# A hybrid mixer layer on one core: normalising the mixer's input early, SiLU in one instruction, and transposes by VectorE and DRAM

## The chip, the core and the metric

The kernel runs on one core of one Trainium2 chip. The metric is the device time of one execution in microseconds (us). The engines are named as the profile names them: PE is TensorE (matmuls, with PEld for its weight loads), DVE is VectorE, ACT is ScalarE, POOL is GpSimd and SP is SyncE, which here issues nearly all DMAs. PSUM is the accumulator memory that PE writes to, and its unit here is a bank of 128 x 512 fp32.

## The reference

One decoder layer on 512 tokens of width 1024, all in fp32:

```python
h = h + 0.5 * swiglu(rmsnorm(h, ffn1_norm[l]), ffn1_w_in[l], ffn1_w_out[l])
h = h + hybrid_mixer(rmsnorm(h, mix_norm[l]), w_in[l], ...)
h = h + 0.5 * swiglu(rmsnorm(h, ffn2_norm[l]), ffn2_w_in[l], ffn2_w_out[l])
return rmsnorm(h, final_norm)
```

The mixer projects the normalised input with one wide matrix and splits the columns:

```python
(hq, hf, hi, hg, gq, gk, gv, ga, gb, gz, gate_h, gate_g) = jnp.split(proj, offsets, axis=-1)
# HGRN2 branch, 8 heads
q_h = silu(hq) * HG_DK ** -0.5;  log_f, k_h from hf
o_h = rmsnorm(hgrn2_chunked(q_h, k_h, hi, log_f), hgrn_out_norm) * silu(hg)
# Gated DeltaNet branch, 8 q/k heads, 16 value heads
qkv = silu(causal_short_conv(concat([gq, gk, gv]), conv_w))      # 4 taps
q_g, k_g = l2norm per head;  beta = sigmoid(gb);  g = -exp(a_log) * softplus(ga + dt_bias)
o_g = rmsnorm(gated_delta_chunked(q_g, k_g, cv, beta, g), gdn_out_norm) * silu(gz)
y = sigmoid(gate_h) * (o_h @ w_branch_hgrn) + sigmoid(gate_g) * (o_g @ w_branch_gdn)
return y @ w_out
```

The delta rule inverts, for each chunk and value head, a unit lower triangular matrix `I + A`, where `A` comes from `k k^T`, beta and the decays. Then a recurrence over the chunks reads and updates a 128 x 128 state per head.

## The kernel before

**Layout.** Activations lie with channels on the 128 partitions and the 512 tokens along the free axis ("channel-major"). `h` holds 8 such tiles (`h[:, kt]`). Every large matmul is done in three passes of a split fp32: the weights become `whi` and `wlo`, the activations `uh` and `ul`, and `mm3` (lines 165 to 168) issues hi*hi, hi*lo and lo*hi. ACT makes `whi` (a cast) and DVE makes `wlo` (a subtraction) from each 256 KB slab that SP has loaded into one of three `raw` buffers. Six `whi`/`wlo` pairs let the slabs be made ahead of PE.

**Stages.** The first feed-forward layer ends near 358 us, the mixer follows up to about 1258 us, then the second feed-forward layer. In the mixer a product of one 128-column block of the weights takes 24 matmuls of 512 columns into one of the two `mm` banks. The letters of the string `DENSE` name these products: F and Q (forget gate and query of an HGRN2 head), B (value and output gate of two HGRN2 heads, tokens on partitions), D (the decays), k, q, v (inputs of the convolution), y (HGRN2 branch projection), z (output gate of two delta heads, tokens on partitions, matmuls of 256 columns). The 16 products `t` (merge gates) are fillers: `choose` takes one when nothing in `DENSE` may go, and keeps two back while something is left there.

**What sets the order.** The class `Desk` plans the mixer when the kernel is built. Each piece of work is a generator that asks for a buffer ("get"), an event ("on"), a time on an engine ("use") or a delay ("lag"). The planner keeps a modelled clock for each engine, gives the engine to the ready piece of the smallest rank, and the instructions come out in that order. On the chip each engine then runs its own list in order and waits on semaphores, so an engine whose next instruction is late holds back everything behind it. SP's DMAs are ordered in the same way.

**Normalisation.** The RMSNorm factor of each token is not ready when the mixer's products start. `uh` and `ul` therefore hold `h` times the norm's gain, without that factor. The function `norm` (lines 1962 to 1989) sums the squares, takes the power on POOL and spreads the factor over the partitions as `rbc`. Each product's result is multiplied by `rbc` when it leaves PSUM (lines 919, 990, 1008, 1218, 1601), or by `rcol`, the factor as a column, where tokens lie on partitions (lines 1027 and 1624).

**SiLU** is made from Tanh: ACT computes `th = tanh(x/2)`, DVE computes `(th + 1) * x`, and the factor 2 left over is taken out later (lines 999, 1234, 1626, and the constants 4.0 at lines 1175, 1288 and 1547).

**Transposes.** The delta rule needs keys and values with tokens on partitions, and its output goes back to channels on partitions. PE does these as four matmuls with an identity each: `ptk` (line 1264, key and query of each of 8 head groups), `ptv` (line 1372, 16 value heads), `pto` (line 1568, 16 outputs) and `pt` (line 1193, 8 HGRN2 outputs).

**Delta rule.** For head group `u` (two value heads): `conv` makes k, q and v; `norms` and `g_n` make the norms and the matrix `n2`; `g_b` writes the 32 x 32 diagonal blocks of `n2` to DRAM (`nb`, line 1343), reads them back broadcast into the one buffer `m` (line 1349), and POOL inverts them in 31 steps of two instructions (lines 1361 and 1362); `g_inv` builds the full inverse; `g_rec` runs the recurrence over four chunks, then normalises and gates the output (line 1560), transposes it and writes it to DRAM (`od`). `operand` reads it back and splits it for the last product, `closing`.

Of the kernel before, what the change touches and what calls it, by code (L numbers as in the profile page):

```python
# [24 lines left out]
HH = 8  # L25
# [16 lines left out]
EXTRA = ((1, 3, 5, 7), (1, 3, 5, 7), (1, 3, 5, 7), (5, 7))  # L42
# [82 lines left out]
def body(tc, xT, cst, sqc, hmask, dta, w1o, w1a, w2a, wt, wn, wab, wbh, wbg, wo, w1b, w2b, yT, dbg=None):  # L125
# [25 lines left out]
    rcol, rhalf = rcols[:, 0:4], rcols[:, 8:12]  # L151
# [665 lines left out]
def mixer(tc, mp, e):  # L817
# [3 lines left out]
    uh, ul, rbc, rcols, rcol, rhalf, h = (e[k] for k in ("uh", "ul", "rbc", "rcols", "rcol", "rhalf", "h"))  # L821
    psc, dr, dense, slab, wp, mm3, ux, hd, dbg = (
        e[k] for k in ("psc", "dr", "dense", "slab", "wp", "mm3", "ux", "hd", "dbg"))
    wt, wn, wab, wbh, wbg, wo, dta, psd = (e[k] for k in ("wt", "wn", "wab", "wbh", "wbg", "wo", "dtab", "psd"))
# [60 lines left out]
    od = dr.tile([VH, P, T], F32, name="od")  # L885


    D = Desk(wx0=1, wx1=1, wx2=1, wx3=1, mm=2, a=2, b=2, d=1, e=1, ta=TA, tm=6, thg=1, raw=RB, w=WB, n2=2, gz=2, fs=1, ut=1, t=3, kn=3, gm=1,
# [15 lines left out]

    def decays(pab):
# [6 lines left out]
        yield "on", "rbc"  # L912
# [5 lines left out]
        yield *V(512), 1  # L918
        dve.tensor_tensor(z, z, rbc[:64], op=ALU.mult)
# [65 lines left out]
    def h_q(i, pt):  # L985
        yield "get", "ta", 2
        yield "on", "rbc"
        yield *V(512), 1
        qs = ta("qs")
        dve.tensor_tensor(qs, pt, rbc, op=ALU.mult)  # L990
        D.put("mm")
        yield A(512)
        th = ta("th")
        act.activation(th, qs, AF.Tanh, scale=0.5)
        tag = ("fs", "ut")[i % 2]
        yield "get", tag, 1
        yield V(512)
        qq = hq[i] = place(tag, "qq", (P, NT, 192), 4)
        dve.scalar_tensor_tensor(qq[:, :, :P], v3(th, NT), 1.0, v3(qs, NT), op0=ALU.add, op1=ALU.mult)
        D.put("ta", 2)  # L1000
        D.fire(("Q", i))

    def h_f(i, pt):
        yield "get", "ta", 1
        yield "on", "rbc"
        yield *V(512), 1
        fs = ta("fs")
        dve.tensor_tensor(fs, pt, rbc, op=ALU.mult)
        D.put("mm")
        yield A(512)  # L1010
        act.activation(fs, fs, AF.Tanh, scale=0.5)
# [13 lines left out]
    def h_v(i, t, o):  # L1025
        yield A(300)
        act.activation(hv_[i][:, t], o, AF.Copy, scale=rcol[:, t:t + 1])
        if t == 3:
            D.fire(("V", i))

    def h_head(i):
# [143 lines left out]
        dve.tensor_scalar(rho, ss, 4.0 / P, 4.0 * EPS * 4.0 * P, op0=ALU.mult, op1=ALU.add)  # L1175
# [4 lines left out]
        yield V(4)  # L1180
        dve.tensor_tensor(rho, rho, rcol, op=ALU.mult)
# [7 lines left out]
        yield "get", "d", 1  # L1189
        yield T_(.46)  # L1190
        pt = ps("pt")
        for c in range(NT):
            pe.transpose(pt[:, c * P:(c + 1) * P], on[:, c], ident)
# [3 lines left out]
        yield A(560)  # L1197
        act.activation(oh, pt, AF.Copy, scale=gn)
        yield V(560)
        dve.scalar_tensor_tensor(ol, pt, gn, oh.bitcast(F32), op0=ALU.mult, op1=ALU.subtract)  # L1200
        D.put("d")
        D.put(tag_o)
# [9 lines left out]
    def conv(k, i, pt, out, n):  # L1212

        yield "get", "ta", 2
        yield *V(512), 1
        ci = ta("ci", (P, T + 32))[:, :T + 3]
        dve.memset(ci[:, :3], 0.0)
        dve.tensor_tensor(ci[:, 3:], pt, rbc, op=ALU.mult)
# [39 lines left out]
    def norms(u, i, kq, kn, sm):  # L1258
# [4 lines left out]
        for c in range(NT):  # L1263
            pe.transpose(pt[:, c * P:(c + 1) * P], kq[:, c, i], ident)
# [848 lines left out]
```

## Time and profile before

| | |
|---|---|
| median of 3 runs | 1624.95 us (1624.8 to 1631.92) |
| profiled execution, its own time | 1623.19 us |
| its span in the profile | 1621.4 us |
| busy share of the span: PE, DVE, ACT, POOL | 99%, 70%, 53%, 26% |
| granted PE clock, mean | 0.997 |
| HBM read, written | 197.45 MB, 17.07 MB |

The span runs from the first to the last instruction; the time of the run lies 1.8 us above it. A busy PE here means that a matmul is in flight. Matmuls overlap, so the price of one is the distance between the starts of two that follow each other and not its own duration.

### The profile page before, as it was taken

Reading aid. Unit: us, or ns where it says so; the run is one execution under the profiler, and the core shown is the slowest. Engines: PE = TensorE matmul, PEld = TensorE weight load, DVE = VectorE, ACT = ScalarE, POOL = GpSimd, SP = SyncE. Lnnn points to the kernel's source line nnn. Section 1 sums busy time; section 2 is a strip of 40 time slices with the busy share of each in tenths; the row PEclk is TensorE's granted clock in tenths of the full one; section 3 lists DMA queues with packets and bytes.
Section 4 is the critical chain, followed back from the end, with each engine's and each line's share of the span. In section 5 each row is a group of like instructions: output and inputs, shape, how many; then the busy total and the mean of one; then the engine's idle time right before and its main releaser. Section 6 shows DMA issues by size and latency. Waiting matters only on the chain.

```text
span 1621.4 us, 30263 instructions
## 1 busy us (share of the span) xinstructions
PE 1599.5 (99%) x11170; PEld 1408.9 (87%) x11170; DVE 1134.0 (70%) x2166; ACT 858.5 (53%) x1853; POOL 414.6 (26%) x744
## 2 busy tenths in 40 slices
PE   8999999999999999999999999999999999999997
PEld 7999998887878788888888988888888899999887
DVE  7877774547677778658888888755545877778353
ACT  7766663332434435456566565553325766667232
POOL 0222210101121221254571666510001322220012
PEclk9999999999999999999999999999999999999999
DMA  5988843532312222443323333445545888883343
GB/s 177 236 185 183 183 104 98 172 114 86 104 40 73 88 76 90 129 147 98 102 90 110 104 102 121 150 137 185 159 143 163 192 201 183 184 185 79 115 136 117
DMA packets 128165, 216.52 MB, mean 134 GB/s; under 512 B 21888, under 2 KB 27776, under 8 KB 128016
## 3 DMA queue, kind: packets, MB, share of 16 engines
q1 hardware_dynamic: 110448, 182.89, 35.6%
q0 software_dynamic: 17280, 31.46, 12.8%
q8 instruction: 88, 1.44, 0.4%
q14 instruction: 61, 0.50, 0.1%
q10 hardware_dynamic: 288, 0.22, 0.1%
HBM read 197.45 MB, written 17.07 MB: 132 GB/s over the span
## 4 chain that ended last, share of the span: by engine, by line
PE 92%; DMA 3%; issue 1%; ACT 1%; DVE 1%; POOL 0%; SPq 0%; DVEq 0%; ACTq 0%; POOLq 0%
PE pmm L166 16%; PE pmm L167 15%; PE pmm L168 15%; PE pnat L166 4%; PE pnat L168 4%; PE pnat L167 4%; PE pfa L166 3%; PE pfa L167 3%; PE pfa L168 3%; PE pfx L166 2%; PE pfx L168 2%; PE pfx L167 2%; PE pfy L168 2%; PE pfy L167 2%; PE pfy L166 2%
## 5 line engine op out<-in xcount | busy, mean ns | idle before, releaser
L166 PE MATMUL pmm<-uh,whi 128*128 128x512 f32 x632 | 264.4, 418 | 5.6 <-ACT whi L709 5.6
L1865 ACT CAST whi<-raw 128x512 fp32r<-128x512 f32 x226 | 140.1, 620 | 214.5 <-PE pmm L167 156.8
L1867 DVE TENSOR_TENSOR wlo<-raw,whi 128x512 fp32r<-128x512 f32 x226 | 160.6, 711 | 128.3 <-ACT whi L1865 121.8
L168 PE MATMUL pmm<-uh,wlo 128*128 128x512 f32 x632 | 248.2, 393 | 0.0
L167 PE MATMUL pmm<-ul,whi 128*128 128x512 f32 x632 | 247.9, 392 | 0.0
L420 DVE TENSOR_TENSOR sig<-h,sig 128x1024 fp32r<-128x1024 f32 x80 | 97.7, 1221 | 70.4 <-ACT sig L418 70.4
L166 PEld LDWEIGHTS pmm<-uh,whi 128*128 128x128 f32 x632 | 119.5, 189 | 27.1 <-ACT whi L709 5.6
L168 PEld LDWEIGHTS pmm<-uh,wlo 128*128 128x128 f32 x632 | 119.2, 189 | 26.3
L166 PE MATMUL pmm<-gh,whi 128*128 128x512 f32 (+1 forms) x374 | 140.9, 377 | 0.0
L168 PE MATMUL pmm<-gh,wlo 128*128 128x512 f32 (+1 forms) x374 | 140.9, 377 | 0.0
L167 PE MATMUL pmm<-gl,whi 128*128 128x512 f32 (+1 forms) x374 | 140.8, 377 | 0.0
L167 PEld LDWEIGHTS pmm<-ul,whi 128*128 128x128 f32 x632 | 119.7, 189 | 20.4 <-DVE ul L193 0.2
L418 ACT CAST sig<-h 128x1024 fp32r<-128x1024 f32 x80 | 83.9, 1049 | 88.1 <-PE pfa L168 85.1
L204 POOL TENSOR_TENSOR acc<-acc,sqt 128x512 f32<-128x512 f32 x18 | 24.1, 1338 | 376.4 <-ACT sqt L202 376.3
L166 PE MATMUL pnat<-whi,uh 128*128 128x256 f32 (+1 forms) x328 | 107.7, 328 | 0.0
L162 DVE TENSOR_TENSOR wlo<-raw,whi 128x512 fp32r<-128x512 f32 x74 | 54.9, 746 | 67.6 <-ACT whi L161 66.9
L168 PE MATMUL pnat<-whi,ul 128*128 128x256 f32 (+1 forms) x328 | 100.6, 307 | 0.0
L167 PE MATMUL pnat<-wlo,uh 128*128 128x256 f32 (+1 forms) x328 | 100.4, 306 | 0.0
L395 POOL DMA_DIRECT2D wlo<-w1b x63 | 54.5, 868 | 145.9 <-ACT s L470 101.3
L168 PE MATMUL pfa<-th,sig 128*128 128x256 f32 x320 | 90.9, 284 | 0.6 <-DVE sig L420 0.5
L166 PE MATMUL pfa<-th,sig 128*128 128x256 f32 x320 | 91.0, 284 | 0.4 <-ACT s L475 0.4
L167 PE MATMUL pfa<-tl,sig 128*128 128x256 f32 x320 | 90.7, 283 | 0.0
(489 smaller groups left out, 4566.1 us busy)
## 6 DMA issues: line engine op xcount, KB each, us to landing
raw<-wt SPq DMA_DIRECT2D x128, 256.0 KB
raw<-w1b SPq DMA_DIRECT2D x88, 256.0 KB
raw<-w1a SPq DMA_DIRECT2D x80, 256.0 KB
raw<-wn SPq DMA_DIRECT2D x64, 256.0 KB
wlo<-w1b POOLq DMA_DIRECT2D x63, 256.0 KB, 5.9
wlo<-w1a POOLq DMA_DIRECT2D x57, 256.0 KB, 5.5
raw<-w2b SPq DMA_DIRECT2D x45, 256.0 KB
raw<-w2a SPq DMA_DIRECT2D x40, 256.0 KB
```

The source lines that it names most:

```text
L162: dve.tensor_tensor(lo[:, :f], raw[:, :f], hi[:, :f].bitcast(F32), op=ALU.subtract)
L166: pe.matmul(pt, ah, bh, start=first, stop=False, **kw)
L167: pe.matmul(pt, ah, bl, start=False, stop=False, **kw)
L168: pe.matmul(pt, al, bh, start=False, stop=last, **kw)
L204: add.tensor_tensor(acc, acc, s, op=ALU.add)
L395: pool.dma_start(lo, src_, accum_op=ALU.add)
L418: act.copy(hl[:, 0:2], s)
L420: dve.tensor_tensor(hl[:, 2:4], s, hl[:, 0:2].bitcast(F32), op=ALU.subtract)
L1865: act.copy(hi, raw)
L1867: dve.tensor_tensor(lo, raw, hi.bitcast(F32), op=ALU.subtract)
```

## The change

The input of the mixer's products is normalised, all but four of them. A new product `S0` runs the four blocks F0, Q0, F1 and Q1 together on the input without the factor, with the eight input tiles in the outer loop and four banks (`mm` twice, `a` twice). Behind each of its eight steps, `renorm` rewrites that tile of `uh` and `ul` with the factor in. The product `B0` then runs over four banks with the same outer loop. All later results leave PSUM without a multiplication by `rbc` or `rcol`.

SiLU becomes one ACT instruction with the function Silu, in `h_q`, `conv`, `gate` and the new `zgate`. The convolution reads its input straight from PSUM: ACT makes the last tap, and three DVE instructions with shifted columns add the others, where the bank was free before after one DVE instruction.

Fifty groups of four PE transposes go: the keys and queries (16), the values (16), the delta outputs of the first seven head groups (14) and the outputs of the first four HGRN2 heads (4). In their place `turned` transposes 32 x 32 blocks on DVE and writes the tile to DRAM, and `regroup` reads it back with four DMAs whose runs are 32 fp32, that is 128 bytes. The gate `z` is now computed channel-major in 16 products of 512 columns, passed through Silu, kept in DRAM (`zd`), and multiplied in by `operand`; its 16 products join the 16 `t` as fillers, ahead of them. The delta outputs are scaled by their norm on ACT.

In the delta rule `n2` has three buffers instead of two, `m` has two instead of one, DVE makes `n2` from PSUM without the copy `gm`, and the two Exp of a head group stand next to each other on ACT.

```diff
 DENSE = (
-    "F0 Q0 F1 Q1 B0 F2 Q2 F3 Q3 B1 D0 F4 Q4 F5 Q5 B2 F6 Q6 F7 Q7 B3 "
-    "k0 q0 k1 q1 y0 y1 y2 y3 v0 v1 y4 y5 y6 y7 k2 q2 v2 v3 z0 k3 q3 v4 v5 z1 k4 q4 v6 v7 z2 "
-    "k5 q5 v8 v9 z3 k6 q6 v10 v11 z4 k7 q7 v12 v13 z5 v14 v15 z6 z7 "
+    "S0 B0 F2 Q2 F3 Q3 B1 D0 F4 Q4 F5 Q5 B2 F6 Q6 F7 Q7 B3 "
+    "k0 q0 k1 q1 y0 y1 y2 y3 v0 v1 y4 y5 y6 y7 k2 q2 v2 v3 k3 q3 v4 v5 k4 q4 v6 v7 "
+    "k5 q5 v8 v9 k6 q6 v10 v11 k7 q7 v12 v13 v14 v15 "
 )
-EXTRA = ((1, 3, 5, 7), (1, 3, 5, 7), (1, 3, 5, 7), (5, 7))
+EXTRA = ((), (1, 3, 5, 7), (1, 3, 5, 7), (5, 7))
...
+    def turned(x, src, mem, then=None, *arg):
+        yield V(512)
+        dve.transpose(v3(x, NT), v3(src, NT) if len(src.shape) < 3 else src)
+        if then is not None:
+            then(*arg)
+        yield S
+        sp.dma_start(mem, x)
+        yield "lag", LAG["out"]
+
+    def regroup(to, mem):
+        rows = mem.rearrange("(t s) (c b r) -> b s c t r", t=4, c=NT, b=4)
+        for b in range(4):
+            yield S
+            o = to[32 * b:32 * b + 32]
+            sp.dma_start(o.rearrange("p (c t r) -> p c t r", c=NT, t=4) if len(o.shape) < 3 else
+                         o.rearrange("p c (t r) -> p c t r", t=4), rows[b])
+        yield "lag", LAG["back"]
...
     def conv(k, i, pt, out, n):
-        yield "get", "ta", 2
-        yield *V(512), 1
-        ci = ta("ci", (P, T + 32))[:, :T + 3]
-        dve.memset(ci[:, :3], 0.0)
-        dve.tensor_tensor(ci[:, 3:], pt, rbc, op=ALU.mult)
-        D.put("mm")
-        yield A(512)
-        y = ta("cy")
-        act.activation(y, ci[:, :T], AF.Copy, scale=wc[0])
-        for j in range(1, 4):
-            yield V(550)
-            dve.scalar_tensor_tensor(y, ci[:, j:j + T], wc[j], y, op0=ALU.mult, op1=ALU.add)
-        yield A(512)
-        th = ci[:, :T]
-        act.activation(th, y, AF.Tanh, scale=0.5)
-        ...
-        dve.scalar_tensor_tensor(out, a, 1.0, b, op0=ALU.add, op1=ALU.mult)
+        yield "get", "ta", 1
+        yield *A(512), 1
+        y = ta("cy")
+        act.activation(y, pt, AF.Copy, scale=wc[3])
+        for j in range(1, 4):
+            yield *V(550), 1
+            dve.scalar_tensor_tensor(y[:, j:], pt[:, :T - j], wc[3 - j], y[:, j:], op0=ALU.mult, op1=ALU.add)
+        D.put("mm")
+        ...
+        if n:
+            act.activation(out, v3(y, n), AF.Silu)
+        else:
+            act.activation(y, y, AF.Silu)
+            D.start((4, k[1], 5), values_of(k, y))
...
     def norms(u, i, kq, kn, sm):
-        yield "get", "e", 1
-        pt = ps("ptk", "e")
-        for c in range(NT):
-            pe.transpose(pt[:, c * P:(c + 1) * P], kq[:, c, i], ident)
+        yield from turned(x, kq[:, :, i], kd[2 * u + i])
+        ...
+        yield from regroup(to, kd[2 * u + i])
...
-        yield "on", *([("P", u - 1)] if u else ["m"])
-        m = G["m"][0]
+        yield "on", *([("P", u - 2)] if u > 1 else [("m2", 0)] if u else ["m"])
+        m = G["m2" if u % 2 else "m"][0]
...
     def g_w(u, i, st):
-        pt = ps("ptv", "e")
-        for c in range(NT):
-            pe.transpose(pt[:, c * P:(c + 1) * P], vb[:, c], ident)
-        dve.tensor_tensor(vb, v3(pt, NT), bc(st["c2"][:, :, i], P), op=ALU.mult)
+        dve.tensor_tensor(vb, vb, bc(st["c2"][:, :, i], P), op=ALU.mult)
...
+    def send(u, i, o):
+        yield "get", "on", 1
+        x = places["on"]("on")
+        yield V(512)
+        dve.transpose(v3(x, NT), o)
+        D.fire(("R", u, i))
+        D.start((6, u), keep(od[2 * u + i], x, "on", ("od", 2 * u + i)))
...
+    def zgate(i, pt):
+        yield "get", "ta", 1
+        yield *A(512), 1
+        z = ta("zg")
+        act.activation(z, pt, AF.Silu)
+        D.put("mm")
+        D.start((6, i), keep(zd[i], z, "ta", ("z", i)))
...
     def operand(k, wait, get, make):
-        yield "on", ("od", k), *([("so", k - 2)] if k > 10 else [])
+        yield "on", ("od", k), *(["projected"] if k > 10 else [])
+        yield "on", ("z", k)
+        ...
-        sp.dma_start(og, od[k])
-        yield "lag", LAG["back"]
+        sp.dma_start(zg, zd[k])
+        yield from regroup(og, od[k])
+        yield *V(560), 1
+        dve.scalar_tensor_tensor(og, og, cs[:, C_GN:C_GN + 1], zg, op0=ALU.mult, op1=ALU.mult)
...
+    def renorm(kt):
+        yield "on", "rbc"
+        yield "get", "ta", 1
+        yield V(560)
+        w = ta("un")
+        dve.scalar_tensor_tensor(w, h[:, kt], cs[:, C_MX + kt:C_MX + kt + 1], rbc, op0=ALU.mult, op1=ALU.mult)
+        yield A(512)
+        act.copy(uh[:, kt], w)
+        yield V(512)
+        dve.tensor_tensor(ul[:, kt], w, uh[:, kt].bitcast(F32), op=ALU.subtract)
...
+            if k == "S":
+                yield "get", "mm", 2
+                yield "get", "a", 2
+                ps_ = [psd.tile(...) for _ in range(2)] + [ps("pmm", "a") for _ in range(2)]
+                for kt in range(KD):
+                    yield "on", ("slab", (x, kt))
+                    for o, pt in enumerate(ps_):
+                        yield T_(.69)
+                        mm3(pt, hi[:, c], lo[:, c], *ux(kt), kt == 0, kt == KD - 1)
+                    D.put("w")
+                    D.start((0, kt), renorm(kt))
+                for o, (th, lane) in enumerate(((h_f, "mm"), (h_q, "mm"), (h_f, "a"), (h_q, "a"))):
+                    D.start((5, n), th(o // 2, ps_[o], lane, True))
+                continue
```

More of the change, by code (lines that the diff above doesn't have):

```diff
@@ L911, in decays @@
         z2 = h[:16, 2]
-        yield "on", "rbc"
         yield A(512)
@@ L1188, in h_head @@
         D.fire(("o", i))
-        yield "get", "d", 1
-        yield T_(.46)
-        pt = ps("pt")
-        for c in range(NT):
-            pe.transpose(pt[:, c * P:(c + 1) * P], on[:, c], ident)
+        if i >= 4:
+            yield "get", "d", 1
+            yield T_(.46)
+            x = ps("pt")
+            for c in range(NT):
+                pe.transpose(x[:, c * P:(c + 1) * P], on[:, c], ident)
+        else:
+            yield "get", "ta", 1
+            x = ta("xo")
+            yield from turned(x, on, ohd[i], D.put, tag_o)
+            yield from regroup(x, ohd[i])
         gn = cs[:, C_HN:C_HN + 1]
@@ L1253, in g_e @@
             D.put("gb")
-            yield A(512)
+        yield "use", "ACT", 3.9
+        for i in range(2):
+            a = G["at"][u % 4 * 2 + i]
             act.activation(a, a, AF.Exp, scale=-1.0)
@@ L2005, in mixer @@
     D.start((6, 0), claim("t64", "t64", 2, (P, 4, 64), True))
+    D.start((6, 0), spare())
     D.start((6, 0), second())
```

375 lines of the change are left out of this document (204 added, 171 removed).

## The prediction

> **What bounds the kernel now.** I read the page first: the busy shares, the slices and the chain that ended last.
>
> ```profile
> span 1621.4 us, 30263 instructions
> PE 1599.5 (99%) x11170; PEld 1408.9 (87%) x11170; DVE 1134.0 (70%) x2166; ACT 858.5 (53%) x1853; POOL 414.6 (26%) x744
> PE   8999999999999999999999999999999999999997
> DVE  7877774547677778658888888755545877778353
> PE 92%; DMA 3%; issue 1%; ACT 1%; DVE 1%; POOL 0%; SPq 0%; DVEq 0%; ACTq 0%; POOLq 0%
> ```
>
> PE is busy in nearly every slice and makes 92% of the chain. The mixer may still have stages of its own, so the next view gives the busy time in stretches of it (columns: stretch, its length, then busy time of PE, PEld, DVE, ACT, POOL, granted clock, DMA share, GB/s). The last three rows are from a second such view over the delta rule alone.
>
> ```profile
> core 0: us, PE busy (x) PEld busy (x) DVE busy (x) ACT busy (x) POOL busy (x), PEclk, DMA share, GB/s
> 360.00:460.00 100.00, 100.00 (x819) 81.57 (x817) 72.00 (x188) 37.41 (x82) 17.20 (x21) 1.00 0.26 80
> 1060.00:1130.00 70.00, 69.09 (x412) 56.78 (x411) 39.03 (x89) 34.27 (x91) 4.13 (x4) 1.00 0.48 166
> sum 900.00, PE 898.66 PEld 757.35 DVE 649.33 ACT 446.48 POOL 284.89; mean PE 99.85 PEld 84.15 DVE 72.15 ACT 49.61 POOL 31.65
> ...
> 764.00:815.00 51.00, 51.00 (x408) 44.13 (x407) 44.79 (x104) 32.69 (x93) 28.75 (x65) 1.00 0.34 100
> sum 402.00, PE 401.56 PEld 349.30 DVE 314.77 ACT 236.28 POOL 215.56; mean PE 50.20 PEld 43.66 DVE 39.35 ACT 29.54 POOL 26.95
> ```
>
> Over the mixer's 900 us PE is busy for 898.66, at the full clock. So **PE's queue is the bound of the mixer**, and the change is worth what it takes out of that queue, less the waits that it puts in. DVE is next: over the eight periods of the delta rule (402 us) it is busy 314.77 / 402 = 78%, and up to 44.79 / 51 = 88%. POOL needs 27 us and PE 50 us per head group, so the inversions don't set the pace.
>
> The merge gates `t` tell how much room the delta chain has at its end. Their row gives the first and last of the 16:
>
> ```profile
> L1601 DVE TENSOR_TENSOR tg<-pmm,rbc x16: 674/684/693, 558.1 to 1128.3; 128x512 f32<-128x512 f32 x16
> ```
>
> The fillers last to 1128 us, until the closing product begins; PE has work in hand to the end.
>
> **Terms on PE.** A busy duration is not the price of a matmul; the distance of starts is. The groups of the transposes and one place each where they stand between dense matmuls (start, duration, what):
>
> ```profile
> L1568 PE MATMUL pto<-sq,on 128*128 128x128 f32 x64 | 9.7, 273 | 0.0
> L166 PE MATMUL pnat<-whi,uh 128*128 128x256 f32 x256 | 77.8, 304 | 0.0
> ...
> 719.26 0.39 PE L167 MATMUL pmm<-ul,whi 128*128 128x512 f32 x1
> 719.49 0.40 PE L168 MATMUL pmm<-uh,wlo 128*128 128x512 f32 x1
> 719.72 0.60 PE L1264 MATMUL ptk<-sq,h 128*128 128x128 f32 x4
> 720.08 0.48 PE L166 MATMUL pmm<-uh,whi 128*128 128x512 f32 x1
> 720.39 0.40 PE L167 MATMUL pmm<-ul,whi 128*128 128x512 f32 x1
> ...
> 781.83 0.28 PE L167 MATMUL pnat<-wlo,uh 128*128 128x256 f32 x1
> 781.95 0.28 PE L168 MATMUL pnat<-whi,ul 128*128 128x256 f32 x1
> ```
>
> Two dense matmuls of 512 columns stand 719.49 - 719.26 = 0.23 us apart (0.227 over longer runs). From 719.49 to 720.39 there are two of them and one group of four transposes: 0.90 - 2 x 0.227 = 0.446 us for the group. The change removes 50 groups: 16 `ptk`, 16 `ptv`, 14 of the 16 `pto`, 4 of the 8 `pt`. **That is 50 x 0.446 = 22.3 us.**
>
> The gate `z` has 768 matmuls of 256 columns, three passes of 256 (the `pnat` row), at 781.95 - 781.83 = 0.12 us: 92.2 us. In the new form it has 16 x 24 = 384 of 512 columns at 0.227: 87.2 us. **5.0 us less.** Nothing is added to PE. `S0` has the matmuls of F0, Q0, F1 and Q1, `B0` keeps its number, and fillers replace fillers. 22.3 + 5.0 = 27.3 us, all on the engine that sets the end.
>
> **The start of the mixer.** PE's first matmul there, the factor's copy, the first result that uses it, the convolution's steps and the weight cast:
>
> ```profile
> 358.08 0.39 PE L166 MATMUL pmm<-uh,whi 128*128 128x512 f32 x1
> ...
> L1987 ACT COPY rbc<-pbc x1: 587/587/587, 366.6 to 366.6; 128x512 f32<-128x512 f32 x1
> L1008 DVE TENSOR_TENSOR fs<-pmm,rbc x8: 671/687/692, 367.2 to 549.4; 128x512 f32<-128x512 f32 x8
> L1226 DVE SCALAR_TENSOR_TENSOR cy<-ci,cs,cy 128x512 f32<-128x512 f32 x96 | 72.9, 762 | 2.1 <-ACT cy L1223 0.7
> L1223 ACT ACTIVATE cy<-ci,cs 128x512 f32<-128x512 f32 x32 | 23.0, 721 | 7.9 <-DVE ci L1218 7.3 <-DVE x L1234 0.5
> L1218 DVE TENSOR_TENSOR ci<-pmm,rbc 128x512 f32<-128x512 f32 x32 | 22.0, 687 | 4.9 <-PE pmm L168 4.3
> L1865 ACT CAST whi<-raw 128x512 fp32r<-128x512 f32 x226 | 140.1, 620 | 214.5 <-PE pmm L167 156.8 <-PE pnat L168 19.2 <-issue 16.9
> ```
>
> `S0` runs from 358 us for 96 x 0.227 = 21.8 us, to 380. The factor is there at 366.6 + 0.6 = 367.2. A `renorm` is two DVE instructions and one on ACT, by the nearest rows 0.76 + 0.62 + 0.69 = 2.1 us, and needs its tile's step of `S0` done (2.7 us each). The first six follow the factor at DVE's 1.45 us each and are ready by 376; the last tile is free at 380 and ready near 383, while `B0` needs it only at its eighth step, 380 + 7 x 2.7 = 399. So PE doesn't wait for it. The cover is `B0`'s outer loop; without it the wait would be 2 to 3 us. One small loss: the second block of `S0` goes into the bank of the last product of the feed-forward layer after 0.7 us instead of 5.4 us, and that bank is free only after one DVE instruction of 0.69 us: 0.7 us. Head 1 starts about 15 us late, as its banks `b` hold `B0` until 402. That moves the heads, not PE, which has 32 fillers of 5.45 us to go on with.
>
> **The delta rule off PE.** Each transposed tile now costs one DVE transpose, one write, four reads. DVE has no 128 x 512 transpose in this profile; it lies between a plain 128 x 512 instruction and twice the largest transpose here:
>
> ```profile
> L1386 DVE STREAM_TRANSPOSE x<-gln 128x256 f32<-128x256 f32 x3 | 2.1, 708 | 0.0
> L1234 DVE SCALAR_TENSOR_TENSOR h<-ci,cy 128x512 f32<-128x512 f32 x12 | 8.3, 692 | 3.2 <-ACT ci L1229 2.9
> L1626 DVE SCALAR_TENSOR_TENSOR ggz<-thg,pnat 128x256 f32<-128x256 f32 x24 | 10.0, 417 | 3.8 <-ACT thg L1624 3.6
> L1560 DVE SCALAR_TENSOR_TENSOR on<-gat,sm,ggz 128x128 f32<-128x128 f32 x24 | 8.9, 416 | 0.1
> ```
>
> So 0.69 to 1.42 us; I take 1.1, as both ends are one element per lane and step with a strided source in the second. Per head group DVE gains six of them and two products in `operand`: 6 x 1.1 + 2 x 0.76 = 8.1 us (5.7 to 10.0). It loses, of four convolutions, the multiplication and the last step, 4 x (0.69 + 0.69); of `z`, four times 0.42; the eight gated scalings, 8 x 0.42; two of `gm`, which have the size of the 0.42 row: 5.5 + 1.7 + 3.4 + 0.8 = 11.4 us. DVE is lighter by 1.4 to 5.7 us of 39, so the engine next in line isn't made the bound. ACT takes the eight small scalings and gives back a copy of 512 columns for the keys and two for the outputs, about nothing in sum.
>
> SiLU and Exp may not share ACT's function table. The loads in this profile:
>
> ```profile
> 485.80 0.61 ACT L1865 CAST wx<-raw 128x512 fp32r<-128x512 f32 x1
> 486.43 1.28 ACT L931 ACT_TABLE_LOAD   x1
> 487.72 0.63 ACT L931 ACTIVATE h<-h 16x512 f32<-16x512 f32 x1
> ```
>
> Two loads per head group and a few around the decays are some 20 x 1.28 = 26 us (0 if no load is needed) on an engine busy 29.5 of 50 us; six slabs made ahead (6 x 2.7 = 16 us of PE) cover each. [...]
>
> The DMAs: a regroup moves 2048 runs of 128 bytes. The block writes of `g_b` have such runs. Two answers on the DMA queue, of 1017.6 to 1019.6 us (1104 of these runs) and of 1024.0 to 1030.6 us (reads from DRAM), and the issue on SP:
>
> ```profile
> DMA packets 1192, 0.31 MB, mean 156 GB/s; under 512 B 1104, under 2 KB 1104, under 8 KB 1192
> q1 hardware_dynamic: 1192, 0.31, 71.9%
> ...
> DMA packets 442, 0.95 MB, mean 144 GB/s; under 512 B 52, under 2 KB 171, under 8 KB 441
> q1 hardware_dynamic: 441, 0.94, 50.9%
> L1343 SPq DMA_DIRECT2D nb<-gn x32: 325/448/1347, 657.7 to 1017.7; - x32
> ```
>
> The first gives 2.0 x 0.719 x 16 / 1192 = 0.019 us of an engine per packet, the second 6.6 x 0.509 x 16 / 441 = 0.12. A regroup keeps the 16 engines for 2.5 us by the first and 15.6 by the second; I take the first, whose runs have the same size. Fifty of them are 125 us, on DMA engines at 26 to 48% in the mixer. SP issues some 290 DMAs more at 0.45 us, 130 us over 700 (1.35 us each, the longest of that row, would be 390 us). The waits behind a late regroup are DVE's or ACT's next slab, with 16 us of cover. I take **3 us** of new waits on PE in sum (0 to 25), some of it in the tail, where operands 11 to 13 are read back only when all products are done, and 11 is needed 4 x 2.7 + 2 = 13 us later, against some 10 us to fetch and make it.
>
> **Sum.** The profiled execution's 1623.2 us: 1623.2 - 22.3 - 5.0 + 0.7 + 3 = 1599.6 us. The median of the runs is 1.8 us above it: **1601 us**.
>
> **Rivals.** (a) *The banks are held too long: slower.* A convolution now frees its bank after 0.72 + 3 x 0.76 = 3.0 us in place of 0.69, and PE is back at that bank 24 x 0.227 = 5.45 us after the product's end. It decides when more than 2.4 us of other work come between on ACT and DVE. With DVE at 78 to 88%, two foreign instructions of 0.71 us ahead of each tap make 0.72 + 3 x (0.76 + 1.42) = 7.3 us, 1.8 us over, for 32 convolutions 58 us: 1601 + 58 = 1659 us. Against it: the taps have the highest rank in the plan, and small matmuls stand between the products. 9%. (b) *Short runs are slow to read: slower.* At 15.6 us a regroup takes 50 x 15.6 = 780 us of the DMA engines, more than the idle half of the mixer's 900, so the weights come late as well; it decides from some 9 us per regroup (450 us), and 50 times 1 us on PE is my price: 1601 + 50 = 1651 us. The rows of 0.019 us speak against it. 5%. [...] (c) *The gain is eaten by scattered waits*, no change: fifty round trips and 32 held banks each cost PE 0.3 us, 82 x 0.3 = 25 us, which is 1624 us. 12%. (d) *The change doesn't take PE's work away*, because the transposes only filled waits: the stretches show 1.3 us of idle PE in 900, so there were none to fill. 2%, 1623 us. (e) *Somewhat more*: the 1.3 us of idle PE goes as well and no new wait comes, 1601 - 3 - 1.3 = 1597 us; it is in the forecast's own range.
>
> **How the numbers follow.** Forecast with its own range of 1594 to 1612: 72%. Rivals (c) and (d) lie near 1624, (a) and (b) between 1635 and 1660. Each end leaves out about a tenth: 1593 to 1626. What a measurement can tell from no change is 0.5%, 8 us. Faster by more than that (under 1617): 72% and a part of (c), 0.77. Within: 0.11. Slower: 0.12.
>
> **What would show it.** The groups `ptk` and `ptv` gone, 8 matmuls of `pto` and 16 of `pt` left; PE's busy sum in the mixer down by 25 to 28 us at the same busy share. Wrong would be: PE idle ahead of `pmm` matmuls, released by DVE `cy` (rival a) or by DMA (rival b); idle PE near 380 us; fillers used up before the last recurrence, with PE idle between the last `t` and the closing product; a regroup over 5 us long.

## The result, and the profile after

The changed kernel takes 1616.03 us (median of 5 runs, 1612.69 to 1616.82) against 1624.95 us of the kernel before beside it. The ratio is 0.9937, with a 95% interval of 0.9925 to 0.9949. That is 8.9 us faster, where 24 us were forecast.

The page of the changed kernel: span, busy times, PE's slices, the packets, and the chain that ended last.

```profile
span 1614.9 us, 29415 instructions
...
PE 1580.5 (98%) x10586; PEld 1371.3 (85%) x10586; DVE 1076.1 (67%) x1970; ACT 872.8 (54%) x1905; POOL 388.3 (24%) x736
...
PE   8899999999999999999999999999999999999997
...
DMA packets 241538, 243.73 MB, mean 151 GB/s; under 512 B 128352, under 2 KB 134240, under 8 KB 241392
...
PE 83%; DMA 5%; ACT 4%; DVE 2%; SPq 2%; issue 2%; POOL 1%; POOLq 0%; ACTq 0%; DVEq 0%
```

PE lost 584 matmul records and 19 us of busy time. But it makes only 83% of the chain now, where it made 92%. DMA, ACT, DVE and SP's queue have come into it. The stretches of the mixer, as in the prediction's second view (the two worst of nine rows, and the sum):

```profile
660.00:760.00 100.00, 97.42 (x521) 79.50 (x521) 61.74 (x121) 57.30 (x128) 45.28 (x126) 0.98 0.62 179
...
960.00:1060.00 100.00, 94.51 (x603) 77.72 (x603) 57.07 (x133) 55.08 (x162) 47.75 (x127) 0.97 0.63 169
...
sum 900.00, PE 888.42 PEld 726.87 DVE 599.17 ACT 466.94 POOL 261.48; mean PE 98.71 PEld 80.76 DVE 66.57 ACT 51.88 POOL 29.05
```

PE is idle for 11.6 of 900 us, where it was idle for 1.3. Its clock isn't full in these two stretches either. The waits of PE in the delta rule (engine, line, what it waited for: sum, times, longest) name three places:

```profile
PE pks L1539 <- DVE s L1579: 3.8, 2, 3.0
PE pgq L1366 <- DVE gn L1374: 2.6, 1, 2.6
PE pog L1566 <- DVE gwe L1557: 2.5, 1, 2.5
```

Behind each of them stands a DMA. At the first (start, duration, line; in brackets the idle time and what ended it):

```profile
680.82 0.40 SPq L1902 DMA_DIRECT2D raw<-wt  x1
...
684.51 6.64 SPq L1902 DMA_DIRECT2D raw<-wt  x3
687.78 0.62 ACT L1945 CAST whi<-raw 128x512 fp32r<-128x512 f32 x1 [4.02 <-DMA raw<-wt]
...
688.43 0.69 DVE L1947 TENSOR_TENSOR wlo<-raw,whi 128x512 fp32r<-128x512 f32 x1 [3.95 <-ACT whi L1945]
...
690.72 0.85 DVE L1374 SCALAR_TENSOR_TENSOR gn<-pgq,sm,gat 128x128 f32<-128x128 f32 x3
```

ACT's cast at 687.78 needs the slab of weights that SP issued at 680.82 us. By the updates of its semaphore in the trace this slab is there at 687.68. ACT waits 4.02 us for it and DVE waits 3.95 us for ACT. The small `gn`, which PE's next matmul needs, stands behind that slab on DVE. At the second place (964 us) ACT's square of `norms` waits 3.9 us for a regroup. At the third (1009 us) DVE's product of `operand` waits 4.0 us for one. All three have the same form: an engine's list holds a late tile, and a small instruction of the delta chain is behind it.

Right after each of these waits PE's clock is halved for 3.4 us (columns as before; the clock is the third number from the end):

```profile
692.00:695.40 3.40, 3.40 (x9) 2.66 (x9) 1.89 (x7) 0.00 (x0) 2.69 (x10) 0.52 0.66 222
968.30:971.70 3.40, 3.40 (x39) 2.85 (x39) 2.65 (x10) 2.81 (x13) 2.77 (x9) 0.51 0.67 224
1012.70:1016.10 3.40, 3.40 (x9) 2.22 (x7) 2.91 (x7) 1.36 (x5) 2.93 (x7) 0.50 0.82 249
```

Each costs about 1.7 us, 5.1 us in sum. PE counts as busy then, so the busy time doesn't show it.

From the starts of the matmuls, the mixer (end of the first feed-forward layer to the first matmul of the last projection) took 856.7 us before and 848.0 us after: 8.6 us less instead of the 27.3 us that were forecast to leave PE's queue. Of the missing 18.7 us, 10.3 are idle PE (11.6 - 1.3) and 5.1 are half clock. The other 3.3 us show neither as idle time nor in the clock. Matmuls overlap (a dense one of 512 columns lasts 0.39 us, and the next starts after 0.23 us), so short delays can hide in a busy PE; whether the 3.3 us are such delays, or work that the forecast left out, isn't shown.

### The profile page after: what moved, and what is told of

It reads as the page before. It is cut to its first block, busy times and chain, and to the rows that moved or that the text cites. A ratio compares the mean times of both kernels' runs of the same rounds, so it can differ in the third digit from the quotient of the medians.

```text
span 1614.9 us, 29415 instructions
## 1 busy us (share of the span) xinstructions
PE 1580.5 (98%) x10586; PEld 1371.3 (85%) x10586; DVE 1076.1 (67%) x1970; ACT 872.8 (54%) x1905; POOL 388.3 (24%) x736
## 3 DMA queue, kind: packets, MB, share of 16 engines
q8 instruction: 83, 1.36, 0.3%
## 4 chain that ended last, share of the span: by engine, by line
PE 83%; DMA 5%; ACT 4%; DVE 2%; SPq 2%; issue 2%; POOL 1%; POOLq 0%; ACTq 0%; DVEq 0%
PE pmm L166 15%; PE pmm L167 15%; PE pmm L168 15%; PE pfa L166 3%; PE pfa L168 3%; PE pfa L167 3%; PE pfx L166 2%; PE pfx L167 2%; PE pfx L168 2%; PE pfy L168 2%; PE pfy L166 2%; PE pfy L167 2%; PE pnat L166 2%; PE pnat L168 2%; PE pnat L167 2%
## 5 line engine op out<-in xcount | busy, mean ns | idle before, releaser
L166 PE MATMUL pmm<-uh,whi 128*128 128x512 f32 x760 | 318.8, 420 | 6.8 <-ACT whi L709 5.5
L167 PE MATMUL pmm<-ul,whi 128*128 128x512 f32 x760 | 298.6, 393 | 0.5 <-DVE ul L1713 0.2
L168 PE MATMUL pmm<-uh,wlo 128*128 128x512 f32 x760 | 299.0, 393 | 0.0
L1945 ACT CAST whi<-raw 128x512 fp32r<-128x512 f32 x230 | 142.3, 620 | 232.4 <-PE pmm L167 176.9
L166 PEld LDWEIGHTS pmm<-uh,whi 128*128 128x128 f32 x760 | 143.9, 189 | 35.6 <-ACT whi L709 5.5
L168 PEld LDWEIGHTS pmm<-uh,wlo 128*128 128x128 f32 x760 | 143.6, 189 | 31.8
L167 PEld LDWEIGHTS pmm<-ul,whi 128*128 128x128 f32 x760 | 144.2, 190 | 26.8 <-DVE ul L1632 0.5
L161 ACT CAST whi<-raw 128x512 fp32r<-128x512 f32 x74 | 43.9, 594 | 87.0 <-PE pmm L167 77.6
L386 ACT ACTIVATE wlo<-raw 128x512 fp32r<-128x512 f32 x120 | 75.2, 626 | 26.2 <-PE pfa L168 13.3
L395 POOL DMA_DIRECT2D wlo<-w1a x57 | 49.5, 870 | 135.2 <-ACT s L470 95.8
```

The lines of the kernel that those rows point to most:

```text
L161: act.copy(hi[:, :f], raw[:, :f])
L166: pe.matmul(pt, ah, bh, start=first, stop=False, **kw)
L167: pe.matmul(pt, ah, bl, start=False, stop=False, **kw)
L168: pe.matmul(pt, al, bh, start=False, stop=last, **kw)
L386: act.activation(lo, raw, AF.Copy, scale=-1.0)
L395: pool.dma_start(lo, src_, accum_op=ALU.add)
```

## The experiments

All times are medians; the ratio is to the kernel before on the same chip. "Runs" are the contiguous pieces that a regroup reads. The kernel before had medians from 1624.95 to 1626.33 us on these chips, and the runs of one changed kernel spread by up to 9 us (with Tanh, from 1614.8 to 1623.4), so a difference of a few microseconds between two rows says little.

| what differs from the changed kernel | us | ratio [95%] |
|---|---|---|
| whole rows of 2 KB, four reads | 1602.6 | 0.9858 [0.9845, 0.9871] |
| whole rows, one read | 1604.6 | 0.9874 [0.9859, 0.9889] |
| Tanh in place of the decays' Exp | 1619.1 | 0.9959 [0.9943, 0.9975] |
| planner: issue 0.65 us and landing 9 us | 1607.2 | 0.9891 [0.9877, 0.9905] |
| planner: issue alone | 1620.7 | 0.9958 [0.9944, 0.9971] |
| planner: landing alone | 1616.2 | 0.9938 [0.9925, 0.9950] |
| planner: small matmuls put 1.7 us later | 1712.9 | 1.0530 [1.0515, 1.0544] |
| runs of 512 bytes, 42 of 50 trips | 1604.8 | 0.9869 [0.9855, 0.9882] |
| the same, with both planner figures | 1609.6 | 0.9898 [0.9885, 0.9912] |
| 512 bytes for the outputs alone | 1614.4 | 0.9918 [0.9905, 0.9930] |
| 512 bytes for queries and values alone | 1606.6 | 0.9873 [0.9858, 0.9888] |
| the values' scaling on ACT alone | 1611.6 | 0.9913 [0.9900, 0.9926] |
| whole rows, 200 DMAs more that SP waits in | 1919.7 | 1.1810 [1.1794, 1.1826] |
| whole rows, 200 DMAs more without a wait | 1639.4 | 1.0085 [1.0072, 1.0097] |
| 39 writes issued by ACT | 1613.2 | 0.9926 [0.9912, 0.9941] |
| 512 bytes and these writes by ACT | 1604.5 | 0.9867 [0.9852, 0.9882] |

### Long runs, and one read instead of four

```diff
     def regroup(to, mem):
-        rows = mem.rearrange("(t s) (c b r) -> b s c t r", t=4, c=NT, b=4)
+        rows = mem.rearrange("(b s) (c t r) -> b s c t r", b=4, c=NT, t=4)
```

The second kernel reads the whole tile with a single DMA, at the place of the fourth.

> The four reads of each regroup keep their place and their bytes, but read whole rows (2 KB runs) in place of 128-byte runs, so the rows that come back are in another arrangement; every engine's order is that of the changed kernel. Theory A (PE waits because round trips through DRAM land late, and the DMA engines' time for the short runs makes them late): the reads take 0.7 us of the 16 engines instead of 1.7, the DMA share in the delta rule falls from 0.62 to about 0.50, PE's idle time in the mixer from 11.6 us to under 5, the time from 1616 to 1603 to 1607 us. Theory B (late by the number of DMAs that SP must issue and by the trip itself): idle stays at 8 to 12 us and the time at 1612 to 1617 us. Theory C (loads of ACT's function table): no change, 1613 to 1617 us.

> Each regroup is one DMA that reads the whole tile in 2 KB rows, at the place of the last of the four, so the rows that come back are in another arrangement; every engine's order is that of the changed kernel, but SP issues 150 DMAs less. Theory A and theory B both: idle PE in the mixer under 5 us, 1601 to 1606 us. If only this one and not the reads with long runs gets there, it is B. Theory C: 1613 to 1617 us.

With whole rows and the same order of instructions, 13.4 us come back (1616.0 - 1602.6), and the time is within 2 us of the forecast. The rows come back in another arrangement, so neither kernel computes the layer's result. The transfers' bytes and the engines' order are those of the changed kernel; the second has 150 DMAs less. The time is theory A's, but whole rows shorten SP's issues as well as the packets' time, and the last experiments have to take these apart. The issue of a regroup on SP, in the changed kernel (count: shortest/median/longest, ns):

```profile
L925 SPq DMA_DIRECT2D og<-od x56: 558/634/1382, 969.6 to 1130.1; - x56
```

and the same group with whole rows. Of the three waits there, `pgq` is gone and `pog` is down to 0.8 us; `pks` keeps 2.6 us. PE's idle time in the 900 us is 7.4 us, of which 2.3 us lie behind the mixer (it ends earlier here), and its clock is full throughout the mixer:

```profile
L925 SPq DMA_DIRECT2D og<-od x56: 302/421/546, 963.1 to 1117.8; - x56
```

```profile
PE pks L1539 <- DVE s L1579: 2.6, 1, 2.6
PE pog L1566 <- DVE gwe L1557: 0.8, 1, 0.8
PE pog L1568 <- ACT x L1509: 0.7, 1, 0.7
```

```profile
960.00:1060.00 100.00, 96.76 (x655) 79.73 (x655) 58.57 (x138) 57.74 (x167) 46.18 (x118) 1.00 0.57 175
...
sum 900.00, PE 892.65 PEld 732.95 DVE 607.02 ACT 476.12 POOL 267.90; mean PE 99.18 PEld 81.44 DVE 67.45 ACT 52.90 POOL 29.77
```

The slab of the first place is issued like this with whole rows:

```profile
677.14 0.38 SPq L1902 DMA_DIRECT2D raw<-wt  x1
```

SP issues the same 1011 DMAs in the same order in this kernel and in the changed one, and just before this place PE's matmuls start at the same time in both, within 0.2 us. Yet SP is 3.7 us earlier here (677.14 against 680.82). From issue to landing the slab then takes 6.3 us here and 6.9 us there. Of the 4.2 us by which it is late in the changed kernel, SP's list makes 3.7.

A single read takes 150 issues more off SP and gains nothing further. So the number of DMAs is no loss in itself once the runs are long. The bytes aren't either, since they are the same in all three kernels.

### The table loads

```diff
-            act.activation(a, a, AF.Exp, scale=-1.0)
+            act.activation(a, a, AF.Tanh, scale=-1.0)
```

> The decay matrices of the delta rule take Tanh in place of Exp, which leaves the decay out of them; 16 loads of ACT's function table (16 x 1.28 = 20.5 us of ACT) go, the order of the engines stays. Theory C: PE's waits shrink, 1604 to 1609 us. Theories A and B: the table loads have cover, 1613 to 1617 us, and the three long waits of PE (2.5 us and more) stand where they were.

The loads between Silu and Exp are gone, and the kernel isn't faster than the changed one; its median is 3 us higher, within the spread of its runs. The loads lie under cover, as forecast.

### The planner's figures

```diff
-LAG = dict(raw=3.5, gb=6.5, nb=6, m=7, out=5, back=6)
+LAG = dict(raw=3.5, gb=6.5, nb=6, m=7, out=5, back=9)
...
         for b in range(4):
-            yield S
+            yield "use", "SP", 0.65
```

> Only the planner's figures change: an issue of a regroup's DMA counts 0.65 us on SP (0.63 measured) in place of 0.4, and the delay until its data are there 9 us in place of 6; the order of all engines is planned anew. Theories A and B: what uses a regroup stands later in DVE's and ACT's lists and no longer holds them, idle PE in the mixer under 6 us, 1602 to 1609 us. Theory C: no gain, 1612 to 1620 us.

> Only the planner's figure for the issue of a regroup's DMA on SP, 0.65 us instead of 0.4 us; the order of the instructions follows from it. Everything is computed. With both figures changed the kernel took 1607.2 us. Theory S (SP's queue runs late because its issues are planned too short): most of those 8.8 us, 1607 to 1610 us. Theory L (what is planned too short is the time until the data has landed): 1613 to 1617 us.

> Only the planner's figure for the time from a regroup's last issue to its data, 9 us instead of 6 us. Everything is computed. Theory S (the issues on SP are what is planned too short): 1613 to 1617 us. Theory L (the landing is what is planned too short, so that ACT and DVE are put in front of a tile that is not there and hold up the next slab of weights): 1607 to 1610 us.

Both figures together give 8.8 us, but neither alone gives anything: with the issue alone the median is 4.7 us higher (the intervals overlap). So both theories fail, and the gain of the pair can't be read as the worth of truer figures. Each change makes another order, and each order has its own accidents. In the kernel with the issue figure alone, one of them costs PE 9.4 us:

```profile
667.75 7.05 SPq L917 DMA_DIRECT2D kd<-ggz  x2
673.74 0.71 DVE L913 STREAM_TRANSPOSE ggz<-h 128x512 f32<-128x512 f32 x1 [7.50 <-DMA vd<-ggz]
675.14 0.79 PE L167 MATMUL pmm<-oh,whi 128*128 128x512 f32 x1 [9.37 <-DVE oh L1228]
```

DVE waits for an earlier tile of `turned` to be written before it may fill its buffer again, and PE's operand is behind it. For the changed kernel too, an order-only difference of 5 to 9 us in either direction is thus possible.

```diff
-SLACK = 0.8
+SLACK = 2.5
```

> The changed kernel with one figure of the planner changed: a small matmul of the delta rule is put into PE's list 2.5 us after its operands are modelled to be ready, instead of 0.8 us. All transfers and their runs stay. Everything is computed. If PE loses its time because small matmuls stand in its list ahead of late operands (two of the three long waits are of this kind), 5 to 10 us come back: 1606 to 1611 us. If the lateness is larger than the 1.7 us of added margin or the weights' slabs are what is late, 1614 to 1618 us; a longer chain of the delta rule could also cost PE its work at the end, over 1618 us.

This goes far the other way. Its last stretches of the mixer:

```profile
1060.00:1130.00 70.00, 51.45 (x320) 40.22 (x320) 47.50 (x116) 38.05 (x129) 24.07 (x65) 0.88 0.55 139
1130.00:1260.00 130.00, 96.79 (x512) 74.25 (x513) 63.35 (x132) 48.37 (x143) 25.32 (x65) 0.75 0.49 128
```

The delta chain gets so long that the fillers run out (the last `t` leaves PSUM at 1089.7 us), and PE then waits at many small matmuls, at a clock of 0.88 and 0.75.

### Runs of 512 bytes

The tile is stored in another order in DRAM, and the consumers read it in that order. The keys, whose tile goes to PE as weights, keep 128 bytes.

```diff
-        dve.transpose(v3(x, NT), v3(src, NT) if len(src.shape) < 3 else src)
+        dve.transpose(v3(x, NT) if fine else x.rearrange("p (b c r) -> p c b r", b=4, c=NT),
+                      v3(src, NT) if len(src.shape) < 3 else src)
...
+        rows = mem.rearrange("(t s) (b q) -> b s t q", t=4, b=4)
+        for b in range(4):
+            sp.dma_start(to[32 * b:32 * b + 32].rearrange("p (t q) -> p t q", t=4), rows[b])
...
-        dve.tensor_tensor(vb, vb, bc(st["c2"][:, :, i], P), op=ALU.mult)
+        for c in range(NT):
+            act.activation(swap(vb)[:, c], swap(vb)[:, c], AF.Copy, scale=st["c2"][:, c, i:i + 1])
```

> The transposed tiles are stored in DRAM as (token block or channel block, chunk, 32), so that 42 of the 50 round trips are read back in runs of 512 bytes instead of 128; the eight trips of the keys keep 128 bytes. The consumers read the tile in that order; the scaling of the values by c2 goes from one DVE instruction to four on ACT. Everything is computed. Theory A (the price of a round trip is the length of its runs): 42/50 of the 13.4 us that whole rows of 2 KB gave back, 11 us, so 1605 us (1602 to 1608). Rival A2 (512 bytes are still short runs, or the whole rows gained because their arrangement skips work of the DMA engines elsewhere): under half of it, 1611 to 1616 us.

> The runs of 512 bytes (42 of 50 trips) together with both planner figures (0.65 us per issue, 9 us to the landing). Everything is computed. If short runs and short planning are two ways of curing one loss, waits on late round trips, the two gains do not add: 1601 to 1605 us, as the better one alone. If they are two losses, they add: 1605 - 8.8, 1595 to 1598 us.

> Runs of 512 bytes in the 18 round trips of the outputs alone (4 of HGRN2 heads, 14 of the delta rule); keys, queries and values keep runs of 128 bytes. Everything is computed, in the order of the changed kernel. If the loss lies where the outputs come back (of the three long waits of PE one, at 1008.7 us, and the tail at 1134 to 1138 us stand behind reads of the outputs): 6 to 8 of the 11.3 us, so 1608 to 1611 us. If each trip costs alike: 18/42 x 11.3 = 4.8, 1611 us. If it lies with keys, queries and values alone: 1614 to 1617 us.

> Runs of 512 bytes in the 24 round trips of the queries and values alone (with the scaling of the values in four ACT instructions); keys and all outputs keep 128 bytes. Everything is computed. If each trip costs alike: 24/42 x 11.3 = 6.5, 1610 us. If the loss lies with the outputs: 1614 to 1617 us. If it lies with the trips at the head of the delta rule: 1605 to 1607 us.

> The changed kernel with the scaling of the values by c2 in four ACT instructions instead of one on DVE, and all runs at 128 bytes; nothing else. Everything is computed. If the gains of the two kernels with runs of 512 bytes for the values (1604.8 and 1606.6 us) belong to the length of the runs: 1613 to 1619 us, as the changed kernel. If they belong to the instruction's move and the order that follows from it: 1604 to 1609 us.

The first of these computes the whole layer, is 11.3 us faster than the changed kernel and 1.3% faster than the one before. The issue of its regroups is down like that of the whole rows, and PE is idle for 4.3 of the 900 us:

```profile
L943 SPq DMA_DIRECT2D og<-od x56: 303/430/1562, 966.5 to 1116.5; - x56
```

```profile
sum 900.00, PE 895.67 PEld 733.78 DVE 597.00 ACT 495.37 POOL 263.09; mean PE 99.52 PEld 81.53 DVE 66.33 ACT 55.04 POOL 29.23
```

The gain isn't all due to the runs. The move of the values' scaling to ACT gives 4.5 us alone (1611.6), in another order of the work; that lies between its two expectations. Against that kernel, the long runs of queries and values are worth 5.0 us, and those of all 42 trips 6.8 us. The outputs' runs, in an unchanged order, are worth 1.6 us, which is within the spread of that kernel's runs (1609.3 to 1614.8). Their edit has a price of its own, though. The last product reads the outputs in pieces of 32 elements, and such a matmul is slower: in the group `pmm<-sop` it takes 396 ns on average instead of 389, and the starts are 0.233 us apart instead of 0.227. In the profiled executions the idle PE and the half clock cost 5.2 us less than in the changed kernel, but the mixer is only 2.8 us shorter. The rest is about what 432 such matmuls cost, by an estimate from the two distances (432 x 0.006 = 2.6 us). The kernel with all 42 trips pays this as well.

With the planner's two figures on top the kernel is 4.9 us slower again, which is in neither expectation's range. The gains don't add, but the figures also bring another order, so this doesn't tell one loss from two.

### SP's queue, or the landing of the packets

```diff
             sp.dma_start(o.rearrange("p (c t r) -> p c t r", c=NT, t=4) if len(o.shape) < 3 else
                          o.rearrange("p c (t r) -> p c t r", t=4), rows[b])
+            sp.dma_start(xd[len(more_)], ident[:32, :32])
```

The first form of this experiment wrote the added DMA over the place just read.

> As the kernel with whole rows of 2 KB (so the columns of the transposed tiles are in another order than the reference's), with one short DMA more behind each of the four reads of a round trip: 32 rows of 128 bytes, into a place that the read has just written. That is 200 DMAs more on SP, each with some 0.3 to 0.5 us of issue, where the short runs of 128 bytes add 0.2 us to each of 200 issues; the packets grow by 6400 instead of 102000 or so. Theory A1 (what the short runs cost is SP's time for the longer issues): at least the 13.4 us come back, 1616 us or more. Theory A2 (it is the time of the packets on the DMA engines and in the queue, until the data has landed): 1602 to 1607 us.

> As the kernel with whole rows of 2 KB (so the columns of the transposed tiles are in another order than the reference's), with one DMA more behind each of the four reads of a round trip, from a constant to a place in DRAM of its own, 32 runs of 128 bytes, so that SP waits for nothing: 200 issues of some 0.3 us, 60 us of SP in all, where the runs of 128 bytes add 0.2 us to each of 200 issues, 42 us. Theory A1 (what the short runs cost is SP's time for the longer issues): 1614 us or more. Theory A2 (it is the packets' time until the data has landed): 1602 to 1606 us.

The first form says nothing on the question. SP waits for the landing of each read before it may write there again, about 2 us each time:

```profile
1017.28 0.41 SPq L925 DMA_DIRECT2D x<-vd  x1
1019.16 0.30 SPq L927 DMA_DIRECT2D x<-vd  x1
1019.51 0.41 SPq L925 DMA_DIRECT2D x<-vd  x1
1021.50 0.30 SPq L927 DMA_DIRECT2D x<-vd  x1
```

It shows what a held SP does, though: 317 us more than with whole rows alone. The second form waits for nothing. Its added issues, and then its waits of PE:

```profile
L929 SPq DMA_DIRECT2D xd<-sq x200: 302/419/1735, 445.3 to 1154.3; - x100
```

```profile
PE pks L1543 <- DVE s L1583: 11.9, 3, 6.8
PE pgq L1370 <- DVE gn L1378: 4.7, 1, 4.7
PE pog L1570 <- DVE gwe L1561: 4.7, 2, 4.2
```

Here the reads have whole rows, and the packets grow by some 9600 (not 6400, as I expected) where the short runs add some 96000. Still the same three matmuls wait as in the changed kernel, and longer: the kernel takes 36.8 us more than with whole rows. The added issues are 200 x 0.42 = 84 us of SP, so a microsecond of SP costs 0.44 us. The runs of 128 bytes add 200 x 0.21 = 42 us to SP, which by that rate is 18 us, against the 13.4 us measured. By this estimate SP's time suffices for the loss of the short runs. The rate isn't constant, however: 150 issues fewer than with whole rows gained nothing.

From the other side, 39 writes go from SP's list to ACT's (for `tag == "ta"` in `keep`):

```diff
-        sp.dma_start(to, tile_)
+        (act if tag == "ta" else sp).dma_start(to, tile_)
```

> The changed kernel with 39 of its writes to DRAM (the gates t and z and the branch tiles y, all made by ACT) issued by ACT instead of SP, at the same places; all runs stay at 128 bytes. Everything is computed. SP is relieved of 39 x (0.38 + 0.09) = 18 us and of its waits for ACT at these places; ACT gets about as much more. Theory A1 (SP's queue is the price of the short runs): 200 issues more, 100 us of SP with their gaps, cost 37 us, so 18 us give back 5 to 8: 1608 to 1612 us. Theory A2 (the landing of the packets is the price): 1614 to 1618 us, or more if ACT is held up.

> The kernel with 42 round trips in runs of 512 bytes, with the same 39 writes issued by ACT. Everything is computed. SP's issues take 190 us there between 660 and 1060 us instead of 219, and little is left to gain: 1601 to 1605 us by both theories; above 1607 if ACT's own queue is held up by the issues.

With short runs 2.9 us come back, but the runs reach from 1610.2 to 1616.8 us. This falls between the two expectations and decides nothing. With runs of 512 bytes nothing comes back, as both theories have it. The traces of the changed kernel and of the one with whole rows tell the two causes apart better, because SP issues the same DMAs in the same order in both. A DMA's landing is read here as the last update of its semaphore, where that can be told. Between 660 and 1060 us the reads of the regroups land 2.5 us after the end of their issue with short runs and 2.7 us with whole rows (means over 131 of 140 reads); the slabs land 3.2 and 3.1 us after theirs (104 of 109). So the short runs lengthen the issue, and not the landing behind it. Single issues take far longer than the median, up to 1.96 us for the values in the changed kernel; whether the packets hold SP up there stays open.

## Why the prediction was wrong, point by point

- **What leaves PE: right in kind, about a tenth too large.** 27.3 us were forecast. With whole rows the mixer takes 835.5 us, 21.2 less than before, and PE is idle for 5.1 us of it, 3.7 more than before: 24.9 us in sum. In the changed kernel the same count gives 24.0 us (8.6 + 10.3 + 5.1). Where the other 2.4 to 3.3 us are isn't shown. The groups are as listed, 16 matmuls of `pt` and 8 of `pto`, and `z` runs at 512 columns:

```profile
L166 PE MATMUL pnat<-whi,uh 128*128 128x512 f32 x88 | 36.5, 414 | 0.0
...
L1216 PE MATMUL pt<-sq,hon 128*128 128x128 f32 x16 | 2.4, 272 | 0.0
L1623 PE MATMUL pto<-sq,x 128*128 128x128 f32 x4 | 0.6, 272 | 0.0
```

- **The start of the mixer: right in size.** PE waits 0.3 us there (0.7 forecast) and nowhere for `renorm`. Head 1 starts 22 us later, not 15, and no wait of PE follows from it. In that execution the first feed-forward layer, which the change doesn't touch, ended 1.8 us later than before, which is part of the distance to the forecast.
- **DVE: its direction right, its size too careful.** The transpose of 128 x 512 costs 0.70 us, at the lower bound and as much as a plain instruction of that size (0.69 us), not the 1.1 us that I took. Over the eight periods of the delta rule DVE went from 314.77 to 273.68 us, 5.1 us per head group, inside the bounds of 1.4 to 5.7:

```profile
L913 DVE STREAM_TRANSPOSE ggz<-cy 128x512 f32<-128x512 f32 x8 | 5.6, 700 | 2.1 <-ACT cy L1260 2.1
...
sum 402.00, PE 392.63 PEld 322.20 DVE 273.68 ACT 247.88 POOL 191.63; mean PE 49.08 PEld 40.27 DVE 34.21 ACT 30.98 POOL 23.95
```

- **The table loads: right.** They are there, at 1.28 us each and with 0.1 us of idle ACT ahead of the eight in sum, and removing the loads between Silu and Exp gains nothing (1619.1 us against 1616.0):

```profile
L1302 ACT ACT_TABLE_LOAD x8 | 10.3, 1283 | 0.1
```

- **Rival (a), the held banks: didn't happen.** None of PE's named waits is for a tap `cy`.
- **The failed step: the DMAs, and the term of 3 us of new waits.** I costed the runs of 128 bytes by the DMA engines' packets, 2.5 us per regroup, and found room. The room was there: a packet of 128 bytes took 0.013 us (I had 0.019), and the DMA share between 660 and 1060 us rose to between 0.61 and 0.63, from between 0.34 and 0.44, without a later landing than with whole rows. (The least busy stretch before had 24%, not the 26% that I gave.) But it was the wrong resource. On SP I counted 290 issues at 0.45 us, 130 us over 700, and drew no wait from them. The regroups' issues took 0.63 us, and SP's issues between 660 and 1060 us went from 93 to 219 us, by the sum of their durations. All loads of weights are in that same list. So slabs and regroups come some microseconds late, and ACT and DVE, which take their lists in order, pass that on to the delta chain (at the first place ACT waited 4.02 us and DVE 3.95 us). The cover of 16 us that I counted belongs to the slabs. A small instruction of the delta rule behind a slab on DVE has no such cover, since the planner puts its matmul into PE's list 0.8 us after the data.
- **What this step measured.** What stood at 3 us measured 10.3 us of idle PE and 5.1 us of half clock, for which I had no term: 15.4 us, and 18.7 at most with the 3.3 us that can't be told apart. That is inside the range of 0 to 25 that I gave this term, and the measured time lies between the forecast and rival (c). Rival (c) had the form right (scattered waits) and the size too high; rival (b) named short runs but put their price on the DMA engines. My signs of being wrong looked at the dense `pmm` matmuls; the long waits came at small matmuls of the delta rule, where no sign was set.

## What to carry to other kernels

When a change adds DMAs, cost the issuing engine's list first: number times issue time, with the issue time as it is for that shape (here 0.63 us for runs of 128 bytes, 0.42 us for whole rows), and ask what else is in the list. A busy share of 99% on the bound engine shows that there is no slack to win; it doesn't show that the cover reaches the small instructions queued behind the covered work. And where a planner writes the order, a mended figure can move the time by several microseconds either way, so a gain from one such figure needs its neighbours measured before it is believed.

## What the runs showed of the hardware

- Runs of 128 bytes lengthened the issue on SP: 0.63 us for 32 partitions of 16 runs against 0.42 to 0.43 us for runs of 512 bytes or 2 KB, with the same bytes.
- Waits of 2.5 to 3.0 us on PE were each followed by 3.4 us at half the clock (0.50 to 0.52). With whole rows a wait of 2.6 us for `pks` was followed by full clock (1.00), so the wait's length alone doesn't decide. The ten records of the clock in the changed kernel's trace start on a grid of 3.413 us. The idle time of PE within one step of it was 2.58, 2.29 and 2.82 us at the three waits, but 1.50 and 1.10 us for the 2.6 us with whole rows. With a single read a wait of 3.8 us fell into two steps with 1.9 us each, and the clock stayed full. Behind the mixer of the changed kernel, though, a wait of 2.6 us fell into two steps with 1.36 and 1.67 us of idle PE, and 3.4 us at half the clock followed (0.50). So the idle time of one step doesn't decide alone either; what does isn't shown.
- In the last product, matmuls of 512 columns whose moving operand is read in pieces of 32 elements started 0.233 us apart, against 0.227 us without the pieces.
- The regroups' reads landed about as long behind the end of their issue with both lengths of runs: 2.5 us for runs of 128 bytes, 2.7 us for whole rows (means, 64 KB each).
